# A Strassen down projection whose chained weight sums stand four places apart

## The chip, the cores and the metric

The kernel runs on one core of a Trainium2 chip. Its time is the device time of one execution, in microseconds; lower is better. The core has five engines with an instruction queue each: TensorE (PE, matrix products, with the weight load shown apart as PEld), VectorE (DVE), ScalarE (ACT), GpSimd (POOL) and SyncE (SP). Transfers between HBM and the on-chip buffers run on DMA engines; here SP issues the plain loads, and POOL those that add to what is already in the buffer.

## The reference

A trunk of two decoder layers on x of 512 tokens by 1024 features, in float32. Each layer is a mixer and a gated feed-forward network (D_FF = 2816), each followed by a residual and a normalization. The change concerns the last product, the down projection `w_ffn_down` of 2816 x 1024.

```python
def reference(x, w_in, hg_lb_param, ...):
    for l in range(DEPTH):                                   # DEPTH = 2
        proj = x @ w_in[l]
        ...
        o_a = hgrn2_mixer(...)                               # gated linear recurrence, 4 heads
        o_b = nsa_mixer(...)                                 # sparse attention, 8 heads
        mix = jnp.concatenate([o_a, o_b], axis=-1) @ w_out[l]
        x = layer_norm(ALPHA * x + mix, ln1_g[l], ln1_b[l])
        ffn = (jax.nn.silu(x @ w_ffn_gate[l]) * (x @ w_ffn_up[l])) @ w_ffn_down[l]
        x = layer_norm(ALPHA * x + ffn, ln2_g[l], ln2_b[l])
    return x
```

## The kernel before

Every fp32 product is made of three faster ones: each operand is split into a high part (a copy by ACT in a reduced type, `whi` or `hop`) and a low part (the rest, a subtraction by DVE, `wlo` or `hop`), and `mm3` (lines 79 to 81) issues high x high, high x low and low x high into the same PSUM tile. So each weight that PE uses has to be loaded, copied by ACT and subtracted by DVE first.

The feed-forward network makes gate and up first, in a Strassen scheme with seven products for eight (`seven`, whose `stage` loads two weight blocks and their sums), for pairs of hidden blocks. Their results, in 11 pairs of 128-wide hidden blocks `H[j]`, stay on chip: j counts 256 hidden features. The down projection takes the first eight of them two by two (q = 0 to 3) in another Strassen scheme, whose products are summed over q in PSUM, and the last three as plain products.

In the first loop over q there are four products per q, each 12 matmuls of 128x512 (`dprod`): M with the weight block p11, Y, E and Z. M accumulates into ps_h and ps_o, Y into ps_s, E into ps_d and Z into ps_t. The weights of Y, E and Z are sums that are made by DMA in one buffer `s`: SP loads `wd[1, i]`, POOL adds `wd[1, i+1]` (line 1035); that is split for Y. Then POOL adds `wd[0, i]` (line 1069), and the result is split for E; then POOL adds `wd[0, i+1]` (line 1072), split for Z. An accumulation can only start when the split before has read the buffer, and the next split only when the accumulation has landed. On PE the order is M, Y, E, Z for each q, with the first matmuls of a next product between. After the loop V and W are formed from the sums, four output quarters get their part, and the second loop makes the products Q, M' and N per q (weights `s3`, `p12`, `p22`), with plain products from q = 1 on, and then the rest.

The program is handed to a scheduler that orders the instructions of each engine by their dependencies and the priorities set by `tc.high_priority`; it is not free to change the order of the products of one PSUM tile. Buffers are rings by tag: `wh` and `wl` (the split weights) have 3 places, so a weight's split waits until PE has done the product three places ahead; `wr` (loads) has 2, `f` (the sums) 3, `pt` 2, and `a` (large tiles) 11.

Of the kernel before, what the change touches and what calls it, by code (L numbers as in the profile page):

```python
# [34 lines left out]
class Kern:  # L35
# [17 lines left out]
    def load_w(self, src, w=1024, tag=None, pieces=1):  # L53

        nc = self.nc
        raw = self.sb.tile([128, 1024], F32, name="wraw", tag="wr", bufs=2)
        for c in range(0, w, w // pieces):
            nc.sync.dma_start(raw[:, c:c + w // pieces], src[:, c:c + w // pieces])
        if tag is None:
            hi = [self.sb.tile([128, 1024], F32R, name="whi", tag="wh", bufs=3)]  # L60
            lo = [self.sb.tile([128, 1024], F32R, name="wlo", tag="wl", bufs=3)]
            step = 1024
        elif tag == "a":
            b = self.big("wa", F32R).rearrange("p a b -> p (a b)")
            hi, lo, step = [b[:, :1024]], [b[:, 1024:]], 1024
        else:
            hi, lo = ([self.sb.tile([128, 1024], F32R, name="wx", tag=tag[0], bufs=tag[1])] for _ in range(2))
            step = 1024
        with self.tc.high_priority(offset=3000):
            for i in range(0, w, step // pieces):  # L70
                n = min(step // pieces, w - i)
                h, o = (p[i // step][:, i % step:i % step + n] for p in (hi, lo))
                nc.scalar.copy(h, raw[:, i:i + n])  # L73
                nc.vector.tensor_tensor(o, raw[:, i:i + n], h.bitcast(F32), op=OP.subtract)  # L74
        return lambda c, n: (hi[c // step][:, c % step:c % step + n], lo[c // step][:, c % step:c % step + n])
# [15 lines left out]
    def stage(self, sa, sb):  # L91

        nc = self.nc
        with self.tc.high_priority(offset=3000):
            self.turn += 1
            tag, bufs = ("f", 3) if self.turn % 3 == 0 else ("wr", 2)
            a = self.sb.tile([128, 1024], F32, name="wraw", tag=tag, bufs=bufs)
            s1, s3, d = (self.sb.tile([128, 512], F32, name=n, tag=t, bufs=2) for n, t in (("ws1", "st"), ("ws3", "pc"), ("wd", "wd")))
            nc.sync.dma_start(s1, sb[:, 512:])
            nc.sync.dma_start(s3, sa[:, :512])  # L100
            nc.gpsimd.dma_start(s1, sb[:, :512], accum_op=OP.add)
            nc.gpsimd.dma_start(s3, sb[:, :512], accum_op=OP.add)
            nc.sync.dma_start(a, sa)
            nc.sync.dma_start(d, sb[:, 512:])
        return a, s1, s3, d
# [653 lines left out]
    def layer(self, l):  # L759
# [271 lines left out]
        def raw_w(src, plus=None, tag=("wr", 2)):  # L1031
            t = self.sb.tile([128, 1024], F32, name="wraw", tag=tag[0], bufs=tag[1])
            nc.sync.dma_start(t, src)
            if plus is not None:
                nc.gpsimd.dma_start(t, plus, accum_op=OP.add)
            return t
# [5 lines left out]
                    self.mm3(acc[t], r[0][:, k, s], r[1][:, k, s], *(p[:, k * 512:(k + 1) * 512] for p in w),  # L1042
                             start and k == 0, stop and k == 1, skip_group_check=True)


        M = [self.ps(t) for t in "ho"]
        Y, E, Z = ([self.ps(t) for _ in range(2)] for t in "sdt")
        for q in range(QS):
            i = 2 * q
            a, c = H[i], H[i + 1]  # L1050
            r11, r12, r21, r22 = (x[:, :, b * 256:(b + 1) * 256] for x in (a, c) for b in range(2))
            end = q == QS - 1
            with tc.high_priority(offset=3000):
                s = raw_w(wd[1, i], wd[1, i + 1], ("f", 3))
                p11 = raw_w(wd[0, i])
            o11, o1, o22, o2 = places(4)
            split(o11, r11)
            t1 = self.sb.tile([128, 2, 256], F32, name="t1", tag="st", bufs=2)
            with tc.high_priority(offset=3000):
                nc.vector.tensor_tensor(t1, r11, r12, op=OP.subtract)  # L1060
            split(o1, t1)
            with tc.high_priority(offset=3000):
                nc.vector.scalar_tensor_tensor(r11, t1, -1.0, r22, op0=OP.mult, op1=OP.subtract)
            split(o2, r11)
            split(o22, r22)
            dprod(M, split_w(p11), o11, q == 0, False)
            dprod(Y, split_w(s), o1, q == 0, end)
            with tc.high_priority(offset=3000):
                nc.gpsimd.dma_start(s, wd[0, i], accum_op=OP.add)
            dprod(E, split_w(s), o2, q == 0, end)  # L1070
            with tc.high_priority(offset=3000):
                nc.gpsimd.dma_start(s, wd[0, i + 1], accum_op=OP.add)
            dprod(Z, split_w(s), o22, q == 0, end)
        one, two = slice(0, 512), slice(512, 1024)
        V = [self.sb.tile([128, 512], F32, name="dv", tag="pc", bufs=2) for _ in range(2)]
        W = [self.m([128, 512], "dw") for _ in range(2)]
        with tc.high_priority(offset=4000):
            for t in range(2):
                nc.scalar.copy(V[t], E[t])
                nc.vector.tensor_tensor(V[t], M[t], V[t], op=OP.add)  # L1080
                nc.vector.tensor_tensor(W[t], Y[t], V[t], op=OP.add)
        for t in range(2):
            o = rows[2 + t]
            nc.vector.scalar_tensor_tensor(o[:, one], o[:, one], ALPHA, Z[t], op0=OP.mult, op1=OP.add)
            nc.vector.tensor_tensor(o[:, one], o[:, one], W[t], op=OP.add)
            nc.vector.scalar_tensor_tensor(o[:, two], o[:, two], ALPHA, W[t], op0=OP.mult, op1=OP.subtract)
            o = rows[t]
            nc.vector.scalar_tensor_tensor(o[:, two], o[:, two], ALPHA, V[t], op0=OP.mult, op1=OP.subtract)
# [11 lines left out]

        for q in range(QS):
            i = 2 * q
            a, c = H[i], H[i + 1]
            r11, r12, r21, r22 = (x[:, :, b * 256:(b + 1) * 256] for x in (a, c) for b in range(2))
            end = q == QS - 1
            with tc.high_priority(offset=3000):
                s3 = raw_w(wd[0, i], wd[1, i], ("f", 3))
                p12, p22 = raw_w(wd[0, i + 1]), raw_w(wd[1, i + 1])
                nc.vector.tensor_tensor(r12, r22, r12, op=OP.subtract)
            o3, o21, o4 = places(3)  # L1110
            split(o3, r12)
            split(o21, r21)
            with tc.high_priority(offset=3000):
                nc.vector.scalar_tensor_tensor(r11, r11, -1.0, r21, op0=OP.mult, op1=OP.subtract)
            split(o4, r11)
            dprod(Q, split_w(s3), o3, q == 0, end)
            dprod(M, split_w(p12), o21, False, False)
            dprod(N, split_w(p22), o4, q == 0, end)
            if q:
                j = 2 * QS + q - 1  # L1120
                b = self.big("hs", F32R)
                HS[j] = b[:, :2], b[:, 2:]
                split(HS[j], H[j])
                w1[j] = self.load_w(wd[0, j], tag=("at", 4) if q < 3 else ("pt", 2))
                plain(M, j, (0, 1), w1[j], False, end)
# [140 lines left out]
```

## Time and profile before

| | us |
|---|---|
| median of 3 runs (lowest, highest) | 1415.04 (1412.42, 1416.57) |
| the profiled execution | 1413.97 |
| its span | 1412.2 |
| PE busy (share of the span) | 1334.7 (95%) |
| DVE busy | 1013.5 (72%) |
| ACT busy | 748.9 (53%) |
| POOL busy | 190.9 (14%) |

The span is the time from the first to the last instruction of the profiled execution. A busy PE is not one at full speed: beside the busy time the profile gives the clock that it was granted, as a share of full speed, 0.975 in the mean here. The down projection begins at about 556 us in layer 0 and at 1252 us in layer 1. Lines such as L1015 in the profile are lines of the kernel; line 1015 and 1016 are the two halves of every split in the down projection, so the tile's name says which split it is.

### The profile page before, as it was taken

Reading aid. Unit: us, or ns where it says so; the run is one execution under the profiler, and the core shown is the slowest. Engines: PE = TensorE matmul, PEld = TensorE weight load, DVE = VectorE, ACT = ScalarE, POOL = GpSimd, SP = SyncE. Lnnn points to the kernel's source line nnn. Section 1 sums busy time; section 2 is a strip of 40 time slices with the busy share of each in tenths; the row PEclk is TensorE's granted clock in tenths of the full one; section 3 lists DMA queues with packets and bytes.
Section 4 is the critical chain, followed back from the end, with each engine's and each line's share of the span. In section 5 each row is a group of like instructions: output and inputs, shape, how many; then the busy total and the mean of one; then the engine's idle time right before and its main releaser. Section 6 shows DMA issues by size and latency. Waiting matters only on the chain.

```text
span 1412.2 us, 23417 instructions
## 1 busy us (share of the span) xinstructions
PE 1334.7 (95%) x8853; PEld 1211.1 (86%) x8853; DVE 1013.5 (72%) x2005; ACT 748.9 (53%) x1479; POOL 190.9 (14%) x275
## 2 busy tenths in 40 slices
PE   8999999999999999679999999999999999987797
PEld 6988998899999999457899989987899999975576
DVE  4755798865977779546667568887669777793557
ACT  4154877726555556324352568686365555553340
POOL 1130011110111120110011101011001111201101
PEclk9999999999999999889999999999999999998899
DMA  6252113251687884566433221134337778736562
GB/s 226 75 171 98 61 60 113 68 160 41 174 206 178 198 205 105 119 149 179 149 141 117 75 90 59 54 112 104 106 109 182 179 187 200 181 87 146 128 210 79
DMA packets 67682, 186.53 MB, mean 132 GB/s; under 512 B 8176, under 2 KB 8352, under 8 KB 67057
## 3 DMA queue, kind: packets, MB, share of 16 engines
q1 hardware_dynamic: 44640, 124.73, 26.9%
q0 software_dynamic: 21920, 58.47, 20.4%
q10 hardware_dynamic: 1008, 1.84, 0.4%
q8 instruction: 69, 1.13, 0.3%
q14 instruction: 45, 0.36, 0.1%
HBM read 180.76 MB, written 7.10 MB: 133 GB/s over the span
## 4 chain that ended last, share of the span: by engine, by line
PE 53%; DVE 8%; DMA 7%; issue 3%; ACT 2%; POOLq 0%; DVEq 0%; POOL 0%; ACTq 0%
PE ps_d L79 9%; PE ps_d L80 9%; PE ps_d L81 9%; DMA wraw<-in_wd 6%; PE ps_t L81 3%; PE ps_t L80 3%; PE ps_t L79 3%; PE ps_s L80 2%; DVE wlo L1016 2%; PE ps_s L81 2%; PE ps_s L79 2%; ACT whi L1015 1%; PE ps_t L644 1%; DVE hop L1016 1%; PE ps_h L387 1%
## 5 line engine op out<-in xcount | busy, mean ns | idle before, releaser
L113 ACT CAST whi<-wraw 128x512 fp32r<-128x512 f32 x160 | 98.6, 621 | 124.7 <-PE ps_d L80 96.3
L79 PE MATMUL ps_d<-xh,whi 128*128 128x256 f32 (+1 forms) x424 | 141.0, 336 | 1.6 <-ACT gates L494 1.1
L81 PE MATMUL ps_d<-xh,wlo 128*128 128x256 f32 (+1 forms) x424 | 142.4, 336 | 0.0
L80 PE MATMUL ps_d<-xl,whi 128*128 128x256 f32 (+1 forms) x424 | 141.0, 333 | 0.8 <-DVE mv L709 0.8
L114 DVE TENSOR_TENSOR wlo<-wraw,whi 128x512 fp32r<-128x512 f32 x160 | 108.9, 688 | 44.4 <-ACT whi L113 41.6
L81 PE MATMUL ps_d<-th,wlo 128*128 128x256 f32 x480 | 134.4, 285 | 1.6 <-DVE wlo L114 1.6
L80 PE MATMUL ps_d<-tl,whi 128*128 128x256 f32 x480 | 135.8, 285 | 0.0
L79 PE MATMUL ps_d<-th,whi 128*128 128x256 f32 x480 | 134.7, 285 | 0.0
L73 ACT CAST whi<-wraw 128x1024 fp32r<-128x1024 f32 (+1 forms) x68 | 70.7, 1040 | 97.4 <-PE ps_d L80 19.4
L1016 DVE TENSOR_TENSOR wlo<-wraw,whi 128x1024 fp32r<-128x1024 f32 x56 | 67.3, 1222 | 72.7 <-ACT whi L1015 72.6
L74 DVE TENSOR_TENSOR wlo<-wraw,whi 128x1024 fp32r<-128x1024 f32 (+1 forms) x68 | 82.3, 1211 | 50.4 <-ACT whi L73 50.2
L1015 ACT CAST whi<-wraw 128x1024 fp32r<-128x1024 f32 x56 | 56.9, 1047 | 92.9 <-DMA wraw<-in_wd 81.5
L81 PEld LDWEIGHTS ps_d<-th,wlo 128*128 128x128 f32 x480 | 92.1, 194 | 2.0 <-DVE wlo L114 2.0
L80 PEld LDWEIGHTS ps_d<-tl,whi 128*128 128x128 f32 x480 | 93.0, 194 | 0.1
L79 PEld LDWEIGHTS ps_d<-th,whi 128*128 128x128 f32 x480 | 92.2, 194 | 0.6 <-ACT su L133 0.5
L79 PEld LDWEIGHTS ps_d<-xh,whi 128*128 128x128 f32 x424 | 80.6, 191 | 9.0 <-ACT gates L494 1.3
L80 PE MATMUL ps_d<-wlo,xh 128*128 128x256 f32 (+1 forms) x304 | 88.3, 291 | 0.0
L79 PE MATMUL ps_d<-whi,xh 128*128 128x256 f32 (+1 forms) x304 | 88.2, 291 | 0.0
L80 PEld LDWEIGHTS ps_d<-xl,whi 128*128 128x128 f32 x424 | 81.2, 191 | 7.9 <-DVE mv L709 1.3
L81 PE MATMUL ps_d<-whi,xl 128*128 128x256 f32 (+1 forms) x304 | 87.9, 290 | 0.0
L81 PEld LDWEIGHTS ps_d<-xh,wlo 128*128 128x128 f32 x424 | 81.2, 191 | 7.1
L605 ACT ACTIVATE e<-e,mn 128x128 f32<-128x128 f32 (+3 forms) x128 | 71.7, 563 | 23.2 <-DVE mn L603 22.7
(455 smaller groups left out, 4198.9 us busy)
## 6 DMA issues: line engine op xcount, KB each, us to landing
wraw<-in_wd SPq DMA_DIRECT2D x52, 512.0 KB, 4.0
wraw<-in_wd POOLq DMA_DIRECT2D x32, 512.0 KB, 5.8
wraw<-in_wf SPq DMA_DIRECT2D x31, 512.0 KB, 3.3
wraw<-in_wg SPq DMA_DIRECT2D x24, 512.0 KB, 4.5
wraw<-in_wu SPq DMA_DIRECT2D x24, 512.0 KB, 4.6
ws<-in_wg SPq DMA_DIRECT2D x40, 256.0 KB, 3.4
ws<-in_wg POOLq DMA_DIRECT2D x40, 256.0 KB, 4.8
ws<-in_wu SPq DMA_DIRECT2D x40, 256.0 KB, 3.5
```

What stands on the lines that cost most here:

```text
L73: nc.scalar.copy(h, raw[:, i:i + n])
L74: nc.vector.tensor_tensor(o, raw[:, i:i + n], h.bitcast(F32), op=OP.subtract)
L79: first = t.matmul(out, ah, bh, start=start, stop=False, **kw)
L80: t.matmul(out, ah, bl, start=False, stop=False, **kw)
L81: t.matmul(out, al, bh, start=False, stop=stop, **kw)
L113: nc.scalar.copy(h, raw)
L114: nc.vector.tensor_tensor(o, raw, h.bitcast(F32), op=OP.subtract)
L387: nc.tensor.matmul(p2[:, i], S[:, blk(i)], kq(128 * (i + 2), [[2 * w, n], [256 + w, 2], [1, w]]), start=True, stop=True)
L605: nc.scalar.activation(e, e, AF.Exp, bias=mn, scale=-1.0, accum_out=sm)
L644: nc.tensor.transpose(p[:, c:c + 128], E[qt][:, j * 128:(j + 1) * 128], self.ident)
L1015: nc.scalar.copy(dst[0], src)
L1016: nc.vector.tensor_tensor(dst[1], src, dst[0].bitcast(F32), op=OP.subtract)
```

## The change

1. The first loop's body becomes four functions: `first` (the sum, the operands, product Y), `second` (M), `third` (E) and `fourth` (Z), called in a fixed order in which the three products of one q's chain are apart. The accumulation for E is issued behind Y, the one for Z behind E. `fourth(3)` is called in the second loop, behind its first two products, and the additions of Z into the outputs (`outer`) behind N's of q = 0.
2. Three sums are alive in tag `f`; the sum of q = 3 gets a place of the large tag `a`.
3. `load_w` splits in two halves where the tag is at, qs or e (the DMA remains one).
4. In `stage` the third raw block comes from tag `pt` in place of `f`.

```diff
@@ load_w
             step = 1024
+            if tag[0] in ("at", "qs", "e"):
+                pieces = 2
         with self.tc.high_priority(offset=3000):
-            for i in range(0, w, step // pieces):
-                n = min(step // pieces, w - i)
+            part = min(step, w) // pieces
+            for i in range(0, w, part):
+                n = min(part, w - i)
@@ stage
-            tag, bufs = ("f", 3) if self.turn % 3 == 0 else ("wr", 2)
+            tag, bufs = ("wr", 2) if self.turn % 3 else ("pt", 2) if self.turn == 3 else ("f", 3)
@@ layer
+        def first(q):
             with tc.high_priority(offset=3000):
-                s = raw_w(wd[1, i], wd[1, i + 1], ("f", 3))
-                p11 = raw_w(wd[0, i])
+                if q < 3:
+                    s = raw_w(wd[1, 2 * q], wd[1, 2 * q + 1], ("f", 3))
+                else:
+                    s = self.big("ws").rearrange("p a b -> p (a b)")[:, :1024]
+                    nc.sync.dma_start(s, wd[1, 2 * q])
+                    nc.gpsimd.dma_start(s, wd[1, 2 * q + 1], accum_op=OP.add)
...
-            dprod(M, split_w(p11), o11, q == 0, False)
-            dprod(Y, split_w(s), o1, q == 0, end)
+            sums[q] = s
+            dprod(Y, split_w(s), o1, q == 0, q == QS - 1)
             with tc.high_priority(offset=3000):
-                nc.gpsimd.dma_start(s, wd[0, i], accum_op=OP.add)
-            dprod(E, split_w(s), o2, q == 0, end)
-            with tc.high_priority(offset=3000):
-                nc.gpsimd.dma_start(s, wd[0, i + 1], accum_op=OP.add)
-            dprod(Z, split_w(s), o22, q == 0, end)
+                nc.gpsimd.dma_start(s, wd[0, 2 * q], accum_op=OP.add)
+
+        def second(q):
+            with tc.high_priority(offset=3000):
+                p11 = raw_w(wd[0, 2 * q])
+            dprod(M, split_w(p11), ops["11", q], q == 0, False)
+
+        def third(q):
+            o2, ops["22", q] = places(2)
+            split(o2, half[q][0])
+            split(ops["22", q], half[q][3])
+            dprod(E, split_w(sums[q]), o2, q == 0, q == QS - 1)
+            with tc.high_priority(offset=3000):
+                nc.gpsimd.dma_start(sums[q], wd[0, 2 * q + 1], accum_op=OP.add)
+
+        def fourth(q):
+            dprod(Z, split_w(sums[q]), ops["22", q], q == 0, q == QS - 1)
+
+        for f, q in ((first, 0), (first, 1), (second, 0), (first, 2), (third, 0), (second, 1), (first, 3), (third, 1),
+                     (fourth, 0), (second, 2), (third, 2), (fourth, 1), (second, 3), (third, 3), (fourth, 2)):
+            f(q)
...
             dprod(M, split_w(p12), o21, False, False)
+            if q == 0:
+                fourth(QS - 1)
             dprod(N, split_w(p22), o4, q == 0, end)
+            if q == 0:
+                for t in range(2):
+                    outer(t)
```

The lists below show how the instructions of an engine stand, in order; a row is the line, the operation, the tile written and read, the shape, and a count of equal neighbours. First, POOL's queue at layer 0's down projection, before. The `ws_` tile is the last sum of the gate/up stage; L1069 is the accumulation for E, L1072 that for Z, L1035 the sums' first one; `strip` and `cstrip` are loads for the next layer.

```order
L102 DMA ws_6148<-in_wu 128x512
L1069 DMA wraw<-in_wd 128x1024
L325 DMA cstrip<-csd 128x448
L320 DMA strip<-Z 128x512
L1072 DMA wraw<-in_wd 128x1024
L1069 DMA wraw<-in_wd 128x1024
L1035 DMA wraw<-in_wd 128x1024
L1072 DMA wraw<-in_wd 128x1024
L1069 DMA wraw<-in_wd 128x1024
L1035 DMA wraw<-in_wd 128x1024
L1072 DMA wraw<-in_wd 128x1024
L1069 DMA wraw<-in_wd 128x1024
```

After, where the lines are shifted: L1061 is the accumulation into the sum of q = 3, L1074 those for E, L1087 those for Z, L1038 that of the second loop's sums.

```order
L1074 DMA wraw<-in_wd 128x1024
L328 DMA cstrip<-csd 128x448
L1061 DMA ws<-in_wd 128x1024
L1074 DMA wraw<-in_wd 128x1024 x2
L323 DMA strip<-Z 128x512
L1087 DMA wraw<-in_wd 128x1024
L1074 DMA ws<-in_wd 128x1024
L1087 DMA wraw<-in_wd 128x1024
L1038 DMA wraw<-in_wd 128x1024
L1087 DMA wraw<-in_wd 128x1024
L1038 DMA wraw<-in_wd 128x1024
L1087 DMA ws<-in_wd 128x1024
```

E's and Z's accumulations, which alternated per q, now stand as three of E behind each other, with the sum of q = 3 ahead of the second; then Z's come, with one of E or of the second loop between.

Second, PE in the middle of layer 0's first loop, before: from E's last matmuls of q = 1 to the begin of M of the next q. ps_d is E, ps_t Z, ps_h and ps_o are M.

```order
L80 MATMUL ps_d<-wlo,hop 128x512
L81 MATMUL ps_d<-whi,hop 128x512
L79 MATMUL ps_t<-whi,hop 128x512 x2
L79 MATMUL ps_h<-whi,hop 128x512
L79 MATMUL ps_o<-whi,hop 128x512
L80 MATMUL ps_t<-wlo,hop 128x512
L81 MATMUL ps_t<-whi,hop 128x512
L80 MATMUL ps_t<-wlo,hop 128x512
```

After, at E of q = 1, whose first pair stands further ahead: Y's last matmuls of q = 3 (ps_s), then the first pair of Z of q = 0, then the rest of E.

```order
L83 MATMUL ps_s<-wlo,hop 128x512
L84 MATMUL ps_s<-whi,hop 128x512
L82 MATMUL ps_t<-whi,hop 128x512 x2
L83 MATMUL ps_d<-wlo,hop 128x512
L84 MATMUL ps_d<-whi,hop 128x512
L83 MATMUL ps_d<-wlo,hop 128x512
L84 MATMUL ps_d<-whi,hop 128x512
```

Z's first pair stood directly behind the last matmul of E of the same q, with the first matmuls of the next M behind it; now the Z whose pair stands at E of q = 1 is that of q = 0, so that between an E and its own Z there are three other products.

More of the change, by code (lines that the diff above doesn't have):

```diff
@@ L1047, in layer @@
         Y, E, Z = ([self.ps(t) for _ in range(2)] for t in "sdt")
[L1048 to L1052, printed above, removed]
-            with tc.high_priority(offset=3000):
-                s = raw_w(wd[1, i], wd[1, i + 1], ("f", 3))
-                p11 = raw_w(wd[0, i])
-            o11, o1, o22, o2 = places(4)
-            split(o11, r11)
+        half = [[(H[2 * q + e][:, :, b * 256:(b + 1) * 256]) for e in range(2) for b in range(2)] for q in range(QS)]
+        sums, ops = {}, {}
+        def first(q):
+            with tc.high_priority(offset=3000):
+                if q < 3:
[4 more added lines that the diff above has]
+                    nc.gpsimd.dma_start(s, wd[1, 2 * q + 1], accum_op=OP.add)
+            r11, r12, _, r22 = half[q]
+            o1, ops["11", q] = places(2)
             t1 = self.sb.tile([128, 2, 256], F32, name="t1", tag="st", bufs=2)
@@ L1061, in layer @@
             split(o1, t1)
+            split(ops["11", q], r11)
             with tc.high_priority(offset=3000):
                 nc.vector.scalar_tensor_tensor(r11, t1, -1.0, r22, op0=OP.mult, op1=OP.subtract)
-            split(o2, r11)
-            split(o22, r22)
-            dprod(M, split_w(p11), o11, q == 0, False)
-            dprod(Y, split_w(s), o1, q == 0, end)
+            sums[q] = s
+            dprod(Y, split_w(s), o1, q == 0, q == QS - 1)
             with tc.high_priority(offset=3000):
-                nc.gpsimd.dma_start(s, wd[0, i], accum_op=OP.add)
-            dprod(E, split_w(s), o2, q == 0, end)
+                nc.gpsimd.dma_start(s, wd[0, 2 * q], accum_op=OP.add)
+        def second(q):
             with tc.high_priority(offset=3000):
-                nc.gpsimd.dma_start(s, wd[0, i + 1], accum_op=OP.add)
-            dprod(Z, split_w(s), o22, q == 0, end)
+                p11 = raw_w(wd[0, 2 * q])
[12 more added lines that the diff above has]
+            f(q)
         one, two = slice(0, 512), slice(512, 1024)
@@ L1081, in layer, with outer @@
                 nc.vector.tensor_tensor(W[t], Y[t], V[t], op=OP.add)
-        for t in range(2):
+        def outer(t):
             o = rows[2 + t]
@@ L1102, in layer @@
             i = 2 * q
-            a, c = H[i], H[i + 1]
-            r11, r12, r21, r22 = (x[:, :, b * 256:(b + 1) * 256] for x in (a, c) for b in range(2))
+            r11, r12, r21, r22 = half[q]
             end = q == QS - 1
```

## The prediction

> **What bounds the kernel now.** I read the busy page first, then the list of what TensorE (PE) waited for, then windows and the timeline around those waits. The page says PE is busy 95% of the span, so on average it is the bound; the list says where it is not.
>
> ```profile
> PE 1334.7 (95%) x8853; PEld 1211.1 (86%) x8853; DVE 1013.5 (72%) x2005; ACT 748.9 (53%) x1479; POOL 190.9 (14%) x275
> ```
>
> ```profile
> PE ps_t L79 <- ACT whi L1015: 28.2, 8, 4.2
> PE ps_d L79 <- ACT whi L1015: 12.1, 7, 4.1
> ...
> PE ps_d L80 <- DVE wlo L1016: 3.4, 7, 0.5
> ...
> PE ps_s L80 <- DVE wlo L1016: 1.4, 2, 1.0
> ```
>
> Columns: total us, times, longest. The two first entries, 40.3 us in 15 waits, are all in the down projection: ps_d is the sum E and ps_t the sum Z of the first loop, and both wait for the high half (whi, line 1015) of a weight sum. Windows show what these stretches cost in all; in each row the time after the bounds is the length, then busy time of PE, of its weight load, of VectorE (DVE), ScalarE (ACT) and GpSimd (POOL), then PE's granted clock, the DMA share and GB/s. The first two rows reach from M's first product to N's first product, in layers 0 and 1.
>
> ```profile
> 555.90:646.80 90.90, 66.93 (x252) 49.86 (x251) 52.58 (x69) 34.12 (x46) 12.21 (x15) 0.87 0.60 135
> 1252.20:1342.80 90.60, 68.75 (x253) 50.59 (x252) 52.09 (x68) 34.14 (x46) 11.07 (x13) 0.85 0.58 128
> ...
> 555.90:575.00 19.10, 13.47 (x68) 10.69 (x67) 18.26 (x30) 9.47 (x17) 2.87 (x4) 0.93 0.49 115
> 575.00:595.00 20.00, 14.81 (x53) 10.52 (x52) 7.03 (x8) 5.65 (x7) 2.55 (x3) 0.90 0.64 139
> ...
> 646.80:760.00 113.20, 112.98 (x679) 100.34 (x677) 75.55 (x113) 49.08 (x67) 8.15 (x13) 1.00 0.48 158
> ...
> 600.00:610.00 10.00, 9.04 (x34) 7.06 (x33) 2.90 (x4) 2.39 (x3) 1.69 (x2) 0.85 0.91 209
> ...
> 640.00:650.00 10.00, 10.00 (x45) 8.21 (x44) 9.05 (x12) 5.00 (x7) 1.70 (x2) 0.97 0.91 235
> ...
> 380.00:400.00 20.00, 20.00 (x169) 20.00 (x168) 16.84 (x31) 11.62 (x24) 4.28 (x5) 1.00 0.78 201
> ```
>
> So 24 us of each 90.9 us stretch are plain idle, and the clock is 0.87 and 0.85; right behind it (646.8 to 760) PE is full at clock 1.00. PE's timeline prices both:
>
> ```profile
> 555.91 0.50 PE L79 MATMUL ps_h<-whi,hop 128*128 128x512 f32 x1
> ...
> 556.69 0.28 PE L80 MATMUL ps_d<-tl,whi 128*128 128x256 f32 x1
> 556.80 0.28 PE L81 MATMUL ps_d<-th,wlo 128*128 128x256 f32 x1
> ...
> 579.41 1.22 PE L79 MATMUL ps_t<-whi,hop 128*128 128x512 f32 x2 [2.89 <-ACT whi L1015]
> 590.17 0.74 PE L79 MATMUL ps_d<-whi,hop 128*128 128x512 f32 x2 [0.78 <-ACT whi L1015]
> ...
> 591.77 0.40 PE L81 MATMUL ps_d<-whi,hop 128*128 128x512 f32 x1
> 592.01 0.40 PE L80 MATMUL ps_d<-wlo,hop 128*128 128x512 f32 x1
> ...
> 597.93 1.22 PE L79 MATMUL ps_t<-whi,hop 128*128 128x512 f32 x2 [3.93 <-ACT whi L1015]
> ...
> 599.90 0.63 PE L80 MATMUL ps_t<-wlo,hop 128*128 128x512 f32 x1
> 600.33 0.63 PE L81 MATMUL ps_t<-whi,hop 128*128 128x512 f32 x1
> ...
> 604.10 0.39 PE L80 MATMUL ps_h<-wlo,hop 128*128 128x512 f32 x1
> ...
> 608.41 0.39 PE L81 MATMUL ps_s<-whi,hop 128*128 128x512 f32 x1
> ...
> 617.54 1.22 PE L79 MATMUL ps_t<-whi,hop 128*128 128x512 f32 x2 [3.96 <-ACT whi L1015]
> ...
> 636.49 0.73 PE L79 MATMUL ps_t<-whi,hop 128*128 128x512 f32 x2 [4.02 <-ACT whi L1015]
> ...
> 646.81 0.62 PE L79 MATMUL ps_s<-whi,hop 128*128 128x512 f32 x2
> ```
>
> Records overlap, so spacing of starts is what counts. Between 604.10 and 608.41 lie 19 steps: 0.227 us a wide matmul, 12 of them (one product) 2.72 us. After the wait of 3.93 us the spacing is 0.43 (599.90 to 600.33): the matmuls run at half speed for some 5 us. After the wait of 0.78 us it is 0.24 (591.77 to 592.01): a short wait costs itself alone. One q takes 18.5 to 19.6 us now (579.41, 597.93, 617.54), where its four products need 4 x 2.72 = 10.9.
>
> Why PE waits is the chain of a weight sum. It has three values: s for Y, s plus a block for E, that plus a second block for Z, all in one buffer. Each step is: split by ACT and DVE, accumulating DMA on POOL's queue into the same buffer, split again. Rows of ACT, DVE and POOL for E to Z of q=1, and an earlier one from the dense start:
>
> ```profile
> 589.07 1.04 ACT L1015 CAST whi<-wraw 128x1024 fp32r<-128x1024 f32 x1 [3.50 <-DMA wraw<-in_wd]
> ...
> 596.84 2.94 ACT L1015 CAST whi<-wraw 128x1024 fp32r<-128x1024 f32 x3 [6.20 <-DMA wraw<-in_wd]
> ```
>
> ```profile
> 590.15 1.23 DVE L1016 TENSOR_TENSOR wlo<-wraw,whi 128x1024 fp32r<-128x1024 f32 x1 [3.77 <-ACT whi L1015]
> ...
> 597.91 3.50 DVE L1016 TENSOR_TENSOR wlo<-wraw,whi 128x1024 fp32r<-128x1024 f32 x3 [5.94 <-ACT whi L1015]
> ```
>
> ```profile
> 564.79 0.86 POOL L1069 DMA_DIRECT2D wraw<-in_wd  x1 [26.90 <-DVE wlo L1016]
> ...
> 591.67 0.84 POOL L1072 DMA_DIRECT2D wraw<-in_wd  x1 [6.07 <-DVE wlo L1016]
> ```
>
> ```profile
> 570.10 1.04 ACT L1015 CAST whi<-wraw 128x1024 fp32r<-128x1024 f32 x1 [1.58 <-DMA wraw<-in_wd]
> ```
>
> From split to split it is 596.84 - 589.07 = 7.8 us, against 2.72 us of work of the one product between. E and Z stand next to each other in the program, so each step shows nearly whole.
>
> **The change, part by part.** (1) The order. The first loop becomes Y0 Y1 M0 Y2 E0 M1 Y3 E1 Z0 M2 E2 Z1 M3 E3 Z2, with Z3 behind Q0 and M'0 of the second loop. No product is added or removed. The work of the stretch is 18 products x 12 = 216 wide matmuls x 0.227 = 49.0 us, and the 34 narrow ones of the gate/up tail, at 0.12 (556.69 to 556.80), 4.1: 53.1 us. A chain step needs 7.8 us. From Y0 to E0 and from each E to its Z are four places, 10.9 us (from the other Y to their E six or seven): 3.1 us to spare, so no long wait, and without long waits nothing that slows the clock.
>
> What stays of waiting is at the start. DVE is busy 18.26 of the first 19.1 us, the splits of Y0, Y1, M0, Y2 crowd into it, and the whi/wlo buffers are three, so E0's split cannot begin before Y1's matmuls are over. I walked the rows through the new order: about 0.5 us before E0, some tenths before the low halves, and 0 to 2 before Z0, whose accumulation comes out of the crowded part. I put 2 us per layer (bounds: 0, and 5.6, what PE idles now in the first 19.1 us). So 90.9 - 53.1 - 2 = 35.8 us in layer 0, 90.6 - 55.1 = 35.5 in layer 1, 71 in all.
>
> (2) DVE, ACT. They do the same splits in a shorter time. A q of the first loop needs on DVE four wlo (1.14 us apart: three in 3.50 above) and six operations on 128x512 operands at 0.60 (row below, three in 1.89): 8.2 of 10.9 us. DVE is not the bound in steady state, but in the first 20 us it is close.
>
> ```profile
> 572.92 1.89 DVE L1016 TENSOR_TENSOR hop<-h_at,hop 128x512 fp32r<-128x512 f32 x3
> ```
>
> (3) POOL and DMA. POOL's queue is in order. The accumulation of q=3's first sum now stands ahead of E1's. Its load on SP waits until PE has left a buffer of the gate/up stage, whose last narrow matmuls end at about 563; with a load of 4 us the accumulation goes out near 567.5 and holds E1's behind it for 2 to 3 us, which E1, six places behind Y1, does not feel; q=3's own Y comes at about 574, when that sum has landed and been split. Behind that load on SP stand the loads of p11 for q=2 and 3, used from the tenth product on: hidden by the products before. Each accumulation's own 0.85 us on POOL runs beside PE. DMA is the tight resource. For the window 560 to 640:
>
> ```profile
> q0 software_dynamic: 1728, 6.26, 43.1%
> q1 hardware_dynamic: 1057, 3.87, 15.2%
> ```
>
> 43.1% of 80 us for 6.26 MB is 2.9 us of all 16 engines per 512 KB accumulation, 15.2% for 3.87 MB is 1.65 us per load. A q has three of the one and two of the other: 12.0 us against 10.9 of PE. Part of q=0 to 2's sums is loaded before the stretch begins (buffer tag f has three places), which lends some 10 us, so over four q the demand is about 38 to 45 us in 50: near 0.85 share. The windows above show that 0.91 and 209 to 235 GB/s are reached. I take nothing for it (bounds 0 and 1.1 x 4 x 2 = 9 us).
>
> The Trainium skill speaks against packing these accumulations beside a busy VectorE ("SBUF — State Buffer", section "SBUF: two separate sides"): a DMA issued by GpSimd can starve while VectorE holds the port that they share. By that rule the sum would grow as in rival (e). The trace does not bear it out. An accumulation issued at 564.79, while DVE was full, had its split at 570.10, 5.3 us later, and one at 591.67, with DVE busy 7.03 of 20 us, at 596.84, 5.2 us.
>
> (4) load_w's two pieces for tags at, qs, e: 16 more ACT and 16 more DVE instructions. Halves of 128x512 follow at 0.60 on DVE against 1.14 for the whole, 0.06 us more each time: 1 us on DVE, none on PE, whose stage at 646.8 to 760 idles 0.2 us with DVE at 75.55 of 113. It lets a first matmul start some 0.5 us sooner; nothing waits there. (5) The third raw place of the gate/up stage from pt in place of f, once, in layer 0: it stands beside 20.00 of 20 us of PE work (380 to 400): nothing, bounds ±1. (6) The outer adds moved behind N0: eight DVE operations that no product waits for. New instruction order elsewhere, from the scheduler: ±2 us.
>
> Sum: the profiled execution took 1413.97 us (span 1412.2); less 71 and plus 1 to 2 for (4) to (6) it is 1344. The median of the runs is 1.1 above that execution, so 1345.
>
> **Rivals.** (a) Same mechanism, partly eaten: DMAs crowd, and landings grow. The longest landing of a weight of wd now is 9.8 us:
>
> ```profile
>   DMA to landing us min/median/max: 3.4/5.0/9.8
> ```
>
> With all accumulations at 9.8 in place of the 5.2 from 591.67 to 596.84 a step is 12.4 us. The chains interleave, so four places then take 12.4 in place of 10.9: 1.5 x 4 q x 2 layers = 12 us; the DMA time of above alone gives 9, both at most 21: 1354 to 1366. For it: the 12.0 against 10.9. Against: the loads made ahead. (b) The start goes badly: E0, Z0 and Y3 each wait over 2 us behind DVE, the clock falls to half for 5 us once per layer; 8 us per layer more, 1360. For it: DVE at 18.26 of 19.1. (c) Waits go, yet the clock stays low. Then only the idle 24 + 22 us less the 4 left are saved: 1372. Against: at 0.78 us of wait the spacing was 0.24 at once. The Trainium skill's rule ("TensorE: Matmul & The Clock Gate", section "Part 1: The HAM clock gate") puts the fall to half speed after an idle window of about 3.4 us, by which waits under that leave the clock alone; the rows here agree (0.78 and 3.93). (d) Slower: a step so long that four places do not cover it. The place then takes step/4; it equals today's 18.6/4 = 4.65 us when a step takes 18.6 us, so from there on the kernel is slower than now. It could come about if POOL's queue stood behind the q=3 accumulation, for instance if SP's load for it were 10 us late: E1, E2 and Z0 accumulate behind it. Nothing in the rows lands that late (9.8 at most, once), and it would happen once, not at every step; with 45 us lost per layer needed to pass 1417, I give it 3%. (e) A full DVE holds POOL's accumulations back, each by up to one DVE instruction, 1.23 us. Where a step has 3.1 us to spare that is nothing; at the three without (E0, E1 and Z0, early) it adds 3.7 us per layer: 1352. Against: 5.3 and 5.2 us above. (f) The change not doing what it says, the scheduler putting a chain's products together again, is excluded by the instruction order.
>
> **How the numbers follow.** Forecast 1345, chance 0.55 (its own range 1338 to 1352); (a) 0.17; (b) 0.12; (c) 0.05; (e) 0.02; better than forecast, the second loop also gaining since its weights come earlier (1330 to 1338), 0.04; (d) 0.03; between (c) and no change 0.02. The range leaves out (d), most of (c) and the lower half of the better case: 1334 to 1370. Within 0.3% (about 4 us, what a measurement of this kernel can tell from no change) lies only a chance coincidence, 0.01; slower 0.03; faster 0.96.
>
> **What will show it.** Right: in the list of PE's waits, ps_t and ps_d on whi fall from 40.3 us to under 5; Y's first to N's first matmul take 53 to 58 us; clock 0.97 or more there; the DMA share near 0.85; ACT's whi rows in the middle no longer released by a DMA but by PE (the three buffers). Wrong (a): whi still released by the DMA of wraw, waits of 1 to 3 us at E and Z of q=2 and 3. Wrong (b): waits confined to the first 20 us, DVE full. Wrong (c): no waits but spacing 0.43. The prediction as a whole falls if accumulating DMAs, crowded, take over 10 us to land.

## The result, and the profile after

The changed kernel takes 1351.8 us in the median (1349.0 to 1353.65, 4 runs) against 1413.82 (1412.42 to 1416.57) for the kernel before: a ratio of 0.9557, 95% interval 0.9531 to 0.9584. The prediction was 1345 with a range of 1334 to 1370. The span of the profiled execution went from 1412.2 to 1351.9 us, 60.3 less; 71 less was forecast for the two stretches, 69 to 70 in all.

Lines are shifted in the changed kernel: the splits of the down projection are at 1018 (ACT) and 1019 (DVE), the matmuls at 82 to 84, the accumulations at 1061 (q = 3's sum), 1074 (E), 1087 (Z) and 1038 (second loop). First the busy page, then the list of what PE waited for (total, times, longest, in us):

```profile
PE 1311.2 (97%) x8853; PEld 1200.4 (89%) x8853; DVE 1012.4 (75%) x2021; ACT 749.6 (55%) x1495; POOL 192.5 (14%) x275
...
wraw<-in_wd POOLq DMA_DIRECT2D x26, 512.0 KB, 6.7
```

```profile
PE ps_t L82 <- ACT whi L1018: 5.7, 3, 2.2
...
PE ps_s L82 <- ACT whi L1018: 1.6, 3, 0.6
...
PE ps_d L82 <- ACT whi L1018: 0.7, 2, 0.3
```

The 40.3 us of waits for whi at ps_t and ps_d have become 6.4. Windows from Y's first pair to N's first pair in both layers, and one around the worst wait of layer 1:

```profile
553.80:611.33 57.53, 53.30 (x243) 42.05 (x241) 44.08 (x58) 30.67 (x43) 12.32 (x15) 0.99 0.90 216
1223.28:1280.39 57.11, 53.93 (x242) 43.40 (x240) 44.08 (x58) 30.66 (x43) 11.06 (x13) 0.97 0.85 203
1248.00:1258.00 10.00, 7.75 (x27) 5.88 (x26) 4.19 (x4) 3.96 (x5) 0.26 (x1) 0.83 0.90 240
```

The stretch of 90.9 us is 57.5 long, at clock 0.99, with the DMA share up from 0.60 to 0.90. Ten matmuls of Z3 now lie behind N's first pair, 2.3 us that are not in the 57.5; to the end of the same 18 products it is 60.9 us in layer 0 and 59.5 in layer 1, against 90.9 and 90.5 before. To see what is left I went along PE's timeline and took from each distance of starts the matmul's own time (0.227 us for a wide one, 0.12 for a narrow one). Before, what was over summed to 37.8 us in layer 0 and 37.4 in layer 1; after, to 7.8 and 6.4. That makes 61.0 us less in the two stretches, where the span lost 60.3: the rest of the program took 0.7 us longer. The rows that hold most of the 7.8 and 6.4:

```profile
564.95 0.73 PE L82 MATMUL ps_d<-whi,hop 128*128 128x512 f32 x2 [0.33 <-ACT whi L1018]
...
580.34 0.73 PE L82 MATMUL ps_t<-whi,hop 128*128 128x512 f32 x2 [1.39 <-ACT whi L1018]
...
609.86 1.05 PE L82 MATMUL ps_t<-whi,hop 128*128 128x512 f32 x2 [2.02 <-ACT whi L1018]
611.33 1.22 PE L82 MATMUL ps_s<-whi,hop 128*128 128x512 f32 x2 [0.42 <-ACT whi L1018]
612.35 0.63 PE L83 MATMUL ps_t<-wlo,hop 128*128 128x512 f32 x1
612.77 0.63 PE L84 MATMUL ps_t<-whi,hop 128*128 128x512 f32 x1
...
1250.67 0.73 PE L82 MATMUL ps_t<-whi,hop 128*128 128x512 f32 x2 [2.25 <-ACT whi L1018]
...
1252.47 0.63 PE L82 MATMUL ps_d<-whi,hop 128*128 128x512 f32 x1
1252.90 0.63 PE L83 MATMUL ps_d<-wlo,hop 128*128 128x512 f32 x1
```

Two places: Z0, the end of the first chain (1.4 and 2.25 us), and Z3, the end of the last (2.0 us in layer 0); each wait of 2 us brought between 1 and 2 us of half speed behind it (starts 0.42 and 0.43 apart). With the short wait at N behind it, Z3 makes some 4.5 of layer 0's 7.8 us, and Z0 some 4 of layer 1's 6.4. Z0's chain from E0 on, by ACT, DVE and POOL:

```profile
563.85 1.04 ACT L1018 CAST whi<-wraw 128x1024 fp32r<-128x1024 f32 x1
...
579.24 1.04 ACT L1018 CAST whi<-wraw 128x1024 fp32r<-128x1024 f32 x1 [4.64 <-DMA wraw<-in_wd]
```

```profile
569.67 1.21 DVE L1019 TENSOR_TENSOR wlo<-wraw,whi 128x1024 fp32r<-128x1024 f32 x1
```

```profile
571.17 0.86 POOL L1087 DMA_DIRECT2D wraw<-in_wd  x1 [1.76 <-DVE wlo L1019]
...
598.09 0.85 POOL L1038 DMA_DIRECT2D wraw<-in_wd  x1 [10.09 <-DMA wraw<-in_wd]
598.63 1.20 POOL L1087 DMA_DIRECT2D ws<-in_wd  x1
```

From E0's high half to Z0's this step took 15.4 us, twice the 7.8 of before: 5.8 until DVE came to E0's low half, and 8.1 from the issue to Z0's split. The last two POOL rows are Z3's case: its accumulation (the `ws` row) waited in POOL's in-order queue behind that for the second loop's sum of q = 1, which itself stood for its load to land. And once issued, Z's accumulations land later than they did. From issue to landing they take, before (first row, line 1072) and after (second row, line 1087):

```profile
DMA to landing us min/median/max: 5.1/5.2/5.6
...
DMA to landing us min/median/max: 6.8/8.9/10.2
```

### The profile page after: what moved, and what is told of

Same layout as the page of the kernel before. It is cut to its first block, busy times and chain, and to the rows that moved or that the text cites. A ratio compares the mean times of both kernels' runs of the same rounds, so it can differ in the third digit from the quotient of the medians.

```text
span 1351.9 us, 23468 instructions
## 1 busy us (share of the span) xinstructions
PE 1311.2 (97%) x8853; PEld 1200.4 (89%) x8853; DVE 1012.4 (75%) x2021; ACT 749.6 (55%) x1495; POOL 192.5 (14%) x275
## 4 chain that ended last, share of the span: by engine, by line
PE 59%; DVE 5%; DMA 5%; ACT 2%; issue 2%; POOL 0%; POOLq 0%; DVEq 0%; ACTq 0%
PE ps_d L83 10%; PE ps_d L82 10%; PE ps_d L84 10%; PE ps_t L84 3%; PE ps_t L82 3%; PE ps_t L83 3%; DMA wraw<-in_wd 3%; PE ps_s L82 2%; PE ps_s L83 2%; PE ps_s L84 2%; DMA ws<-in_wd 1%; PE ps_t L647 1%; DVE wlo L1019 1%; DVE hop L1019 1%; PE ps_h L390 1%
## 5 line engine op out<-in xcount | busy, mean ns | idle before, releaser
L1019 DVE TENSOR_TENSOR wlo<-wraw,whi 128x1024 fp32r<-128x1024 f32 x50 | 60.6, 1219 | 38.3 <-ACT whi L1018 38.3
L1018 ACT CAST whi<-wraw 128x1024 fp32r<-128x1024 f32 x50 | 52.3, 1051 | 64.1 <-DMA wraw<-in_wd 38.9
```

Source lines behind the costliest of these rows:

```text
L1018: nc.scalar.copy(dst[0], src)
L1019: nc.vector.tensor_tensor(dst[1], src, dst[0].bitcast(F32), op=OP.subtract)
```

## The experiments

Ratios are to the kernel before, timed on the same chip beside each. The theories are named by letters in the texts on record: A, distance in the chain makes the gain; B, the DMA engines are the bound; B2, VectorE's crowded start; C, POOL's queue; D, half speed as a cost of its own; G, ScalarE's queue made before's chains serial.

### The order alone, and the rest alone

```diff
-            if tag[0] in ("at", "qs", "e"):
-                pieces = 2
...
-            tag, bufs = ("wr", 2) if self.turn % 3 else ("pt", 2) if self.turn == 3 else ("f", 3)
+            tag, bufs = ("f", 3) if self.turn % 3 == 0 else ("wr", 2)
```

> The new order alone, without the two pieces in load_w and without the pt place. Theory A (the distance in the chain makes the whole gain): 1352 us, as the changed kernel, within 3 us, with the same waits at Z0 and Z3. Rival (the pieces made part of it, since the first 555 us became 2.1 us shorter): 1354; or, if they cost the 3 us that layer 1's attention became longer: 1349.

1351.2 us, 0.9543 (0.9526 to 0.9561): as the whole change. The reverse, the kernel before with only these two edits:

> The kernel before with only the two pieces in load_w and the pt place. Theory A: between 1412 and 1414 us, PE's waits in the down projection unchanged near 40 us. Rival (they matter by themselves): 1410 or less, or over 1417.

1419.6 us, 1.0023 (1.0006 to 1.0041). That is above A's 1412 to 1414 and, as the rival said, over 1417; but the kernel before itself took 1416.6 beside it, so what the two edits cost by themselves is 0.4% at most. There is no gain in them; the order makes the whole of it.

### The chain itself: without its accumulations, in both orders

```diff
-            with tc.high_priority(offset=3000):
-                nc.gpsimd.dma_start(s, wd[0, 2 * q], accum_op=OP.add)
...
-            with tc.high_priority(offset=3000):
-                nc.gpsimd.dma_start(sums[q], wd[0, 2 * q + 1], accum_op=OP.add)
```

> The changed kernel without the two accumulations of E and Z (both products use the sum of Y): 8 DMAs per layer and the chain are left out, all splits and matmuls stay. Theory A and C (the rest of the loss, 7 us per layer over the matmuls' own time, is landings and POOL's queue): 1338 to 1342 us, no wait over 1 us in the first loop. Rival B2 (the rest is VectorE's crowded start): the waits stay, 1347 us or more.

1343.5 us, 0.949 (0.947 to 0.951), a little over the 1338 to 1342 of A and C, with no wait over 0.4 us in the first loop and 1.4 us in place of 7.8 over the matmuls' own time in layer 0's stretch. The same two DMAs taken out of the kernel before, in its own order:

> The kernel before, in its own order, without the two accumulations of E and Z (both products use the sum of Y). Theory G (the loss of before is one serial chain: the splits of M and Y of the next q stand behind Z's split in ScalarE's queue, so each q's two accumulations follow the other q's): with the accumulations gone the order M Y E Z costs nothing and the time is that of the changed kernel without them, 1340 to 1346 us. Rival (the order loses by itself, through the three buffers of split weights): 1360 us or more.

1344.6 us, 0.9492 (0.9461 to 0.9523): the two orders are equal without the chain. So the some 70 us that before lost, and the 8 that the changed kernel still loses, come with the two accumulating steps; the order M Y E Z costs nothing by itself. The edit takes the chain and the traffic of its DMAs away together; that the traffic is not the bound is shown by the fastest variant below, which keeps all of it and takes 1342.2 us.

### Fewer places between

```diff
-        for f, q in ((first, 0), (first, 1), (second, 0), (first, 2), (third, 0), (second, 1), (first, 3), (third, 1),
-                     (fourth, 0), (second, 2), (third, 2), (fourth, 1), (second, 3), (third, 3), (fourth, 2)):
+        for f, q in ((first, 0), (second, 0), (third, 0), (first, 1), (fourth, 0), (second, 1), (third, 1), (first, 2),
+                     (fourth, 1), (second, 2), (third, 2), (first, 3), (fourth, 2), (second, 3), (third, 3)):
```

> The changed kernel with the first loop in the order Y0 M0 E0 Y1 Z0 M1 E1 Y2 Z1 M2 E2 Y3 Z2 M3 E3, so that E and its Z are two places apart, and Y and its E two or three, in place of four and more. Theory A (a chain step needs 7.8 us, a place gives 2.72): at each Z about 2.4 us of wait, and at 2 us and more 1.7 us of half speed after it; some 16 us per layer in place of the 7 now: 1365 to 1380 us. Rival (any product between is enough): 1350 to 1355. Rival (a step is 12 to 15 us, as Y0 to Z0's in the changed kernel's start): 1390 to 1400.

1374.8 us, 0.9707 (0.968 to 0.9734), inside theory A's 1365 to 1380. PE waits 18.7 us for Z's high half, up to 5.8 at a time:

```profile
PE ps_t L82 <- ACT whi L1018: 18.7, 5, 5.8
```

Two places give some 42 us, four give 62 to 65. The gain follows the distance, not the mere fact of a product between.

### Is the half speed a cost of its own?

```diff
             dprod(E, split_w(s), o2, q == 0, end)
+            if q < 3:
+                for _ in range(10):
+                    nc.tensor.matmul(E[0], zero[:, :128], o2[0].rearrange("p a b -> p (a b)"), start=False, stop=False, skip_group_check=True)
```

The edit behind Y of q = 0 is alike.

> The kernel before with ten matmuls of a zero operand (adding zero) put into the long waits: behind Y of q = 0 and behind E of q = 0 to 2, in both layers: 80 more matmuls of 0.23 us, 18 us of PE work. Theory D (a long wait costs itself and then the half speed after it, and the latter goes when the wait is cut short): after the eight waits the page of before shows 1.7 to 2.7 us of half speed each, 15 to 17 us in all; the chain alone then sets the time: about 1400 us. Rival E (the clock follows the useful load, or falls after the waits for another reason): 1414 to 1418 us. Rival F (the added matmuls stand in the path): 1425 to 1435 us.

1417.5 us, 1.0011 (0.999 to 1.0031): neither D's 1400 nor F's 1425 to 1435. As a test of the sum it is weaker than D's 15 to 17 us, because the added matmuls took only a part of the half speed away. Over both stretches PE's idle time fell from 45.7 to 39.0 us, and what lies over the waits and the matmuls' own time from 29.4 to 23.8. The rows show what became of that gain. PE's waits for a weight sum, then its timeline around E and Z of q = 0 and 1, and E of q = 2:

```profile
PE ps_d L79 <- ACT whi L1015: 15.7, 8, 3.8
PE ps_t L79 <- ACT whi L1015: 15.7, 8, 4.3
```

```profile
570.50 0.73 PE L79 MATMUL ps_d<-whi,hop 128*128 128x512 f32 x2 [1.52 <-ACT whi L1015]
...
574.16 2.43 PE L1078 MATMUL ps_d<-hop,zero 128*128 128x512 f32 x10
...
590.51 0.73 PE L79 MATMUL ps_d<-whi,hop 128*128 128x512 f32 x2 [1.39 <-ACT whi L1015]
...
598.59 0.73 PE L79 MATMUL ps_t<-whi,hop 128*128 128x512 f32 x2 [1.98 <-ACT whi L1015]
...
601.03 0.39 PE L79 MATMUL ps_t<-whi,hop 128*128 128x512 f32 x1
601.26 0.39 PE L80 MATMUL ps_t<-wlo,hop 128*128 128x512 f32 x1
...
610.47 0.73 PE L79 MATMUL ps_d<-whi,hop 128*128 128x512 f32 x2 [2.93 <-ACT whi L1015]
```

After Z1's wait the spacing is 0.23, full speed, and yet E comes every 20.0 us (570.50, 590.51, 610.47), no sooner than before (571.20, 590.17, 609.75): the time saved by the faster matmuls came back as a longer wait at E. All sixteen products E and Z still waited for their high half, so PE was late at none of them, and neither the zero matmuls nor the faster ones set the time there. In the kernel before, the cycle of a q is set by the chain, and the half speed lay beside it. It is a symptom there. In the changed kernel, where PE is the bound, it adds to the time by the distances of starts above; no run takes it away alone.

### Moving the waits that are left

M of q = 2 ahead of Z0, so that Z0 is five places behind E0:

```diff
-                     (fourth, 0), (second, 2), (third, 2), ...
+                     (second, 2), (fourth, 0), (third, 2), ...
```

> The changed kernel with M of q = 2 put ahead of Z of q = 0, so that Z0 stands five places behind E0. Theory A (Z0's wait is the first chain's step being 15 us long in a crowded start, and the half speed after it follows from it): Z0's waits of 1.4 and 2.25 us vanish, and the half speed after the second; 1346 to 1348 us. Rival B (the DMA engines are the bound of the loop): the wait comes back at E2 or Z1, and the time stays at 1351 to 1353.

1354.4 us, 0.9561 (0.9541 to 0.9581): no gain. Z0's wait is gone in both layers, and one of 4.07 and 3.69 us stands at Z2. That is what rival B said, but the place shows another reason. POOL, ACT and PE around it:

```profile
587.53 0.85 POOL L1038 DMA_DIRECT2D wraw<-in_wd  x1 [10.41 <-DMA wraw<-in_wd]
588.07 1.20 POOL L1087 DMA_DIRECT2D wraw<-in_wd  x1
```

```profile
579.52 2.01 ACT L1018 CAST whi<-wraw 128x1024 fp32r<-128x1024 f32 x2 [3.02 <-DMA wraw<-in_wd]
...
599.18 1.04 ACT L1018 CAST whi<-wraw 128x1024 fp32r<-128x1024 f32 x1 [8.84 <-DMA wraw<-in_wd]
```

```profile
600.28 1.22 PE L82 MATMUL ps_t<-whi,hop 128*128 128x512 f32 x2 [4.07 <-ACT whi L1018]
```

E2 was split from 580.5 on and its low half was done at 583.0, but Z2's accumulation (588.07) stood for 5 us behind the one for the second loop's first sum, whose load had not landed. Then it took 11 us to come in. So the queue explains a part; the slow landing is nearer to what rival B says.

VectorE's share, the eight preparations of the second loop put behind E0's low half by a factor that is computed from it:

```diff
+                    nc.vector.tensor_scalar(minus[0], w[1][:, :1].bitcast(F32), 0.0, -1.0, op0=OP.mult, op1=OP.add)
...
-                nc.vector.tensor_tensor(r12, r22, r12, op=OP.subtract)
+                nc.vector.scalar_tensor_tensor(r12, r12, minus[0], r22, op0=OP.mult, op1=OP.add)
...
-                nc.vector.scalar_tensor_tensor(r11, r11, -1.0, r21, op0=OP.mult, op1=OP.subtract)
+                nc.vector.scalar_tensor_tensor(r11, r11, minus[0], r21, op0=OP.mult, op1=OP.subtract)
```

> The changed kernel with VectorE's preparation of the second loop's operands (eight subtractions of 0.6 us) made to come after the low half of E0, by a factor of -1 that is computed from it; nothing else. Theory B2 (VectorE's crowded start makes E0's step to Z0 15 us long: 7 us pass from E0's high half to the end of its low half): the accumulation for Z0 is issued 2 to 3 us sooner, Z0's wait (1.4 and 2.25 us, and 1.75 us of half speed) goes: 1346 to 1349 us. Rival (the landing of 8 to 9 us is the rest, and takes what is gained, since the DMA engines are full there): Z0's wait stays over 1 us, 1350 to 1353 us.

1351.1 us, 0.9538 (0.951 to 0.9566): no change that can be told. Z0's accumulation goes out at 568.54 in place of 571.17 and Z0 waits 0.24 us in layer 0: B2's mechanism is there, though the landing took 9.3 us in place of 8.0, half of what was gained, as the rival said. But 1.9 and 2.6 us of wait stand at Z2 now, whose accumulation is again right behind one of the second loop.

POOL's order. The load of the second loop's sum for q = 1 held until E3 is split:

```diff
+                if q == 1:
+                    nc.vector.tensor_copy(s3[:, :1], lows[QS - 1][:, :1].bitcast(F32))
                 nc.sync.dma_start(s3, wd[0, i])
```

> The changed kernel with the load of the second loop's sum for q = 1 held until E of q = 3 has been split (a one-column copy into its buffer), so that POOL issues the accumulation for Z3 ahead of that for this sum. Theory C (Z3 is late by the 5 us that its accumulation stood behind the other one in POOL's queue): the wait of 2.0 us at Z3 in layer 0 and the half speed after it go, 1347 to 1349 us. Rival B (it lands late since the DMA engines are full): the accumulation is issued near 593.6 but its split still starts at 607 or later, 1351 to 1353 us.

1346.4 us, 0.9506 (0.9489 to 0.9524), the gain of theory C. Z3's accumulation goes out at 592.41 in place of 598.63 and Z3's wait is gone. The size of the gain is in part luck: Z0's waits, which the edit does not aim at, fell from 1.4 to 0.3 us in layer 0 and from 2.25 to nothing in layer 1, and in layer 1 a wait of 4.1 us came at N of q = 1, whose load is behind the held one:

```profile
592.41 0.85 POOL L1089 DMA_DIRECT2D ws<-in_wd  x1 [4.90 <-DVE wraw L1132]
```

```profile
1285.15 1.22 PE L82 MATMUL ps_s<-whi,hop 128*128 128x512 f32 x2 [4.13 <-ACT whi L1018]
```

To take that wait away, the outer adds got their factor from a column made after N0's split, so that they come behind it on VectorE:

```diff
+                    nc.vector.tensor_scalar(alpha, wn[1][:, :1].bitcast(F32), 0.0, ALPHA, op0=OP.mult, op1=OP.add)
...
-            nc.vector.scalar_tensor_tensor(o[:, one], o[:, one], ALPHA, Z[t], op0=OP.mult, op1=OP.add)
+            nc.vector.scalar_tensor_tensor(o[:, one], o[:, one], alpha, Z[t], op0=OP.mult, op1=OP.add)
```

> The kernel with Z3's accumulation first, whose new waits are at the second loop's products of q = 1 (0.8 and 1.3 us in layer 0, 4.1 us in layer 1), because N0's low half stands behind four of the outer adds on VectorE and the load for N1 behind it. Here the outer adds take their factor from a column made after N0's split, so that they come behind it. Theory: N0's split ends 2.4 us sooner, the load for N1 with it; layer 1's wait falls to 1.7 us or less and its half speed goes: 1341 to 1344 us. Rival (the wait is the load's own, behind the others on SP's queue): 1346 to 1348.

1348.0 us, 0.951 (0.9486 to 0.9535), no change. The wait at N1 fell from 4.1 to 1.0 us, as the theory had it, but 2.1 us at Z0 were back: that wait comes and goes with small shifts at the start.

Both moves together: M2 ahead of Z0, and both early sums of the second loop held, q = 0's until E2 and q = 1's until E3 is split:

```diff
-                     (fourth, 0), (second, 2), (third, 2), ...
+                     (second, 2), (fourth, 0), (third, 2), ...
...
+                if q < 2:
+                    nc.vector.tensor_copy(s3[:, :1], lows[q + 2][:, :1].bitcast(F32))
```

> Z0 five places behind E0, and both sums of the second loop held on SP, that of q = 0 until E2 is split and that of q = 1 until E3 is, so that no accumulation of E or Z stands behind one of the second loop. Theory C: the wait of 4 us that M2 first alone moved to Z2 goes, and Z0's stays away; waits in the first loop under 1 us; 1343 to 1346 us. Rival (the held loads come late for Q0 or N1, since SP's queue is in order too): a wait of 2 to 4 us there, 1347 to 1350 us.

1342.2 us, 0.9495 (0.9462 to 0.9529): the fastest, and below the changed kernel, though the intervals only just part. In the profiled execution, the fastest of six (1337.5 to 1351.1 us), the first loop has no wait of 0.5 us. N of q = 1 waits 1.7 us in layer 0 and 0.7 in layer 1, which is a part of what the rival said. The windows from Y's to N's first pair, layers 0 and 1:

```profile
551.15:603.33 52.18, 51.85 (x242) 42.54 (x241) 45.01 (x61) 31.67 (x43) 12.24 (x15) 1.00 0.95 226
1212.08:1264.26 52.18, 51.85 (x242) 42.54 (x241) 45.26 (x62) 31.58 (x43) 11.10 (x13) 1.00 0.93 217
```

The same work in 52.2 us that took 57.5, with PE busy 51.85 and the DMA engines at 0.95: they are nearly full and still not the bound, which speaks against B.

### Only the splits moved

```diff
+            if not end:
+                s2, p11 = load(q + 1)
+                wm, wy = split_w(p11), split_w(s2)
             dprod(Z, split_w(s), o22, q == 0, end)
```

> The kernel before with one thing moved: the splits of the weights of M and Y for q + 1 (and their loads) are written ahead of Z's split of q; the products stay written M, Y, E, Z. The scheduler then puts PE's products as E0 M1 Y1 Z0 E1 ..., with three places from E to its Z and two from Y to its E. Theory G (what made before slow is that in ScalarE's in-order queue the splits of M and Y of the next q stood behind Z's, which waits for a landing, so that the two steps of every q followed those of the q before): most of the gain comes with this alone, 1355 to 1372 us; the waits that stay are at E, two places behind Y. Rival (it needs the order of the products as in the changed kernel): 1395 us or more.

1394.2 us, 0.984 (0.9805 to 0.9875): a third of the gain, so theory G's number is missed by over 20 us, and the rival's 1395 is about met. In the middle of layer 0's loop a q does take less, 14.9 us from E1 over E2 to E3 in place of about 19. Waits stay at E of q = 0 and 2 (14.9 us in all) and at Z of q = 3 (7.8 and 8.2 us). That is the last q: no M and Y of a next one stand between its E and its Z, on PE or in ScalarE's queue.

```profile
582.50 0.61 PE L79 MATMUL ps_d<-whi,hop 128*128 128x512 f32 x2
...
597.44 1.22 PE L79 MATMUL ps_d<-whi,hop 128*128 128x512 f32 x2 [2.81 <-ACT whi L1015]
...
612.36 0.61 PE L79 MATMUL ps_d<-whi,hop 128*128 128x512 f32 x2
...
623.71 1.22 PE L79 MATMUL ps_t<-whi,hop 128*128 128x512 f32 x2 [7.82 <-ACT whi L1015]
```

That ScalarE's queue is what made before's chains serial is thus not shown, since the edit also put products between E and Z on PE; only that the chains did it is.

## Why the prediction was right, and where its numbers were off

- **The bound and the sum's main term.** Held. The stretch needs 53 us of matmuls, distance removes the waits, and the clock returns: the two stretches gave 61.0 us, and the span lost 60.3. The experiment with two places gave a time between, inside the range worked out from the 7.8 us step.
- **The term that was too small: "I put 2 us per layer"** for what stays of waiting. It measured 7.8 and 6.4, above its bound of 5.6. This is the 10 us between 71 and 61. The walk through the new order gave Z0 0 to 2 us; it was 1.4 and 2.25 plus, in layer 1, some 1.5 us of half speed. It took a step as 7.8 us, while in the crowded start it was 15.4: VectorE kept E0's low half back (rival (b)'s mechanism), and 8.1 us passed from issue to split in place of 5.2 (rival (a)'s). Taking VectorE's part away removed Z0's wait, so that mechanism is real, but neither was worth the 9 to 21 us that its rival gave it. The rest is Z3, where the walk did not go.
- **The 3.1 us to spare.** They were counted with a step of 7.8 us, and the step did not stay so. With Z's accumulations landing after 8.9 us in place of 5.2 it is some 11.5 us (an estimate: 7.8 + 3.7), more than the 10.9 of four places. What saved the middle is that a split runs ahead of its product, since the split weights have three places. E2's split began at 583.40, 4.8 us ahead of its matmuls (588.18); Z2's began 13.7 us later, and Z2 (599.06) did not wait:

```profile
583.40 1.05 ACT L1018 CAST whi<-wraw 128x1024 fp32r<-128x1024 f32 x1 [1.63 <-PE ps_d L84]
...
597.09 1.05 ACT L1018 CAST whi<-wraw 128x1024 fp32r<-128x1024 f32 x1 [4.93 <-DMA wraw<-in_wd]
```

The prediction's sum has no such lead in it. That four places were enough is to that extent luck.
- **POOL's queue.** The prediction looked at q = 3's sum in front of E1 and found it harmless, which it was (E1 did not wait), though it went out at 562.81 and not near 567.5. It missed the accumulations of the second loop in front of Z2 and Z3. Their rows were in the printed order; what was not in it is that their loads land late. Rival (d) had the right mechanism with the wrong place, and at 5 us once, not 45. The 45 do not follow from the prediction's own sum either: from 1345 to 1417 are 72 us, 36 per layer.
- **DMA as the tight resource.** Cost per transfer did not grow. For layer 0's stretch after:

```profile
q0 software_dynamic: 1817, 6.62, 60.0%
```

60.0% of 57.5 us for 6.62 MB is 2.7 us per 512 KB, where the prediction had 2.9; the share reached 0.90 and, in the fastest variant, 0.95 with no wait behind it. Landings did grow, as (a) said (the median of all 512 KB accumulations into `wraw` from 5.8 to 6.7 us, that of Z's from 5.2 to 8.9).
- **The half speed.** Rival (c) leaves 29 of the 71 us to the clock (71 less 24 + 22 - 4). As an account of where PE's time went that is right, as a cause it is not: the kernel with the zero matmuls kept more of the clock (0.982 in the mean against 0.975) and gained nothing. Rival (c) was posed on that confusion. The forecast does not suffer, since it summed what the matmuls need and not what the waits cost.
- **Its signs.** The length of the stretch, the clock and the DMA share came as said. The waits of ps_t and ps_d fell to 6.4 us, not under 5. ACT's splits from 583 to 591 were released by PE, but those of Z2 and Z3 by the DMA, which was the sign of rival (a). And two accumulations took over 10 us to land (10.2 and 10.0), by which the prediction as a whole should have fallen; it did not.
- **Pieces, pt, outer adds: nothing, as said.** The scheduler's jitter was put at ±2; layer 1's attention got a wait of 2.3 us at line 888 in the changed kernel that the kernel with the order alone lacks (0.6), at the same total time.

## What to carry to other kernels

A chain that is updated in place (split, accumulate, split) should be priced by its own step and given that many places of independent work; here 7.8 us against 2.72 us per product, and the gain grew from two places to four. Price the step where it will run, not in the quiet middle of the old kernel: at the crowded start it was twice as long, and Z's accumulations landed 3.7 us later once the loop was dense. When a wait is removed, look next at the in-order queue that feeds it: with the chains apart, the accumulations of a later stage stood in front of urgent ones, and the fastest variant is the one that also holds their loads back.

## What was not expected of the hardware

Waits well under the 3.9 us of the prediction's example already lead to half speed. In the kernel before, the wait of 2.89 us in the prediction's own list is followed by it, and one of 2.22 us in layer 1 too:

```profile
581.38 0.63 PE L80 MATMUL ps_t<-wlo,hop 128*128 128x512 f32 x1
581.80 0.63 PE L81 MATMUL ps_t<-whi,hop 128*128 128x512 f32 x1
```

In the changed kernel, after the 2.02 and 2.25 us above the spacing went to 0.42 or 0.43 us, in the second case not at once but 1.4 us after PE had started again; with the zero matmuls in place half speed came after a wait of 1.99 us and not after one of 1.98:

```profile
578.58 0.73 PE L79 MATMUL ps_t<-whi,hop 128*128 128x512 f32 x2 [1.99 <-ACT whi L1015]
...
581.36 0.63 PE L79 MATMUL ps_t<-whi,hop 128*128 128x512 f32 x1
581.79 0.63 PE L80 MATMUL ps_t<-wlo,hop 128*128 128x512 f32 x1
```

So it is not the length of the wait alone. The Trainium skill ("TensorE: Matmul & The Clock Gate", section "Part 1: The HAM clock gate") lets the clock fall after an idle window of about 3.4 us that runs freely of the kernel; that the outcome varies at equal waits would agree with a window of which a wait may fill more or less, but here waits of 2 us, shorter than the window, were enough. The prediction read its rows of 0.78 and 3.93 us as agreeing with this; its row of 2.89 us between them does not. What decides at equal waits stays open.

Two accumulations issued close together did not land alike. Six times in the two down projections of the changed kernel POOL issued one of 512 KB 0.53 or 0.54 us behind another, as at 598.09 and 598.63 above. The first of each pair landed after 5.1 to 5.7 us, the second after 9.0 to 10.2. Z2's and Z3's accumulations are seconds of such pairs, while those of Z0 and Z1, issued alone, landed after 6.8 to 8.8 us. So standing behind one of the second loop seems to cost time in the landing too, beside the wait in the queue; no run tests it apart.
